# The eleventh image's store cut into one transfer of 60 rows and sixteen transfers of 4 rows, in a dilated convolution

## The chip, the core and the metric

The kernel runs on one NeuronCore of a Trainium2 chip. The metric is the device time of one execution in microseconds (us). Three runs of the kernel before gave 126.09, 126.11 and 126.12 us, median 126.11 us.

## The reference

The kernel computes a 3x3 convolution with dilation 2 and a padding of 2, so that the output has the size of the input. There are 16 images of 64 input channels and 64x64 pixels, 128 output channels, all in float32:

```python
for b in range(batch):
    for co in range(c_out):
        for ci in range(c_in):
            for kh in range(k):
                for kw in range(k):
                    output[b, co] += weight[co, ci, kh, kw] * x_pad[b, ci, kh*dilation:kh*dilation+h, kw*dilation:kw*dilation+w]
```

The output is 16 x 128 x 64 x 64 x 4 bytes = 33.55 MB, the input 16.8 MB. One image of the output is 2 MB, and it lies in a partition (an output channel) as 64 rows of 64 float32, 16,384 bytes in one piece, on the chip and in memory alike.

## The kernel before

**Work.** The images go in eight pairs, `pb` = 0 to 7. The two images of a pair sit on partitions 0 to 63 and 64 to 127, and a pair is worked in four units `u` of 16 rows each. For a unit, TensorE sums matmuls into PSUM (line 186), ScalarE copies the term that two row groups share to SBUF (line 204), and VectorE adds PSUM and copy into the output tile `o` (line 209), twice for each unit. GpSimd loads input pairs ahead of time (line 81) and adds up input rows (line 141).

**Output tiles.** `o` holds a whole pair, 128 partitions x 2 images x 64 x 64 float32. The pool `opool` has three buffers, so pair `pb` writes where pair `pb - 3` was, and has to wait until that one's store has landed.

**Stores.** All stores are issued by SyncE (SP) in the order of the program. Pairs 0 to 4 leave as one transfer of 4 MB each (line 221) once their last unit is added. Pairs 5 and 6 (`BOTH = NP - 3` is 5) leave as two transfers of 2 MB, one for each image (line 224, `hb` = 0 and 1). Pair 7 leaves in halves: after its second and after its fourth unit, two transfers of 1 MB. The eleventh image is image 10, `pb` = 5 with `hb` = 0. SP also issues three loads at the start: the weights (line 64) and the first pair of images in two parts (line 75). That makes 16 transfers on SP's queue.

**Completion semaphores.** A transfer tells of its landing by a semaphore that 16 shares add up to. The framework gives SP's transfers eight such semaphores in turn, called DMAHW0 to DMAHW7 in the built program. The ninth transfer gets the first one again, and SP does not issue it before the first transfer has landed; the tenth waits in the same way for the second one, and so on. The trace shows eight semaphore numbers, each used by two of the 16 transfers, and a wait for that number ahead of its second use. In the built program SP's list reads, from the last 4 MB store on:

```
L221 DMACopy out_0_dram<-o4_759 128x2x4096 [waits DVE_49]
L224 DMACopy out_0_dram<-o5_914 128x4096 [waits DMAHW0_49,DVE_49]
L224 DMACopy out_0_dram<-o5_914 128x4096 [waits DMAHW1_49]
L224 DMACopy out_0_dram<-o6_1070 128x4096 [waits DMAHW2_49,DVE_49]
L224 DMACopy out_0_dram<-o6_1070 128x4096 [waits DMAHW3_49]
```

The store of `o4` has DMAHW7; the three loads at the start have DMAHW0, 1 and 2.

Of the kernel before, what the change touches and what calls it, by code (L numbers as in the profile page):

```python
# [10 lines left out]
def kernel(  # L11
# [7 lines left out]
    nc = tc.nc  # L19

    B, CI, H, W = x.shape
# [56 lines left out]
    def load(pb, cuts):  # L78
        x16[pb] = x16pool.tile([P, H, W], f16, tag="x16", name=f"x16_{pb}")
        for lo, hi in zip(cuts, cuts[1:]):  # L80
            nc.gpsimd.dma_start(out=x16[pb][:, lo:hi], in_=x_pair[pb, :, lo:hi])  # L81
# [18 lines left out]
    for name, a in (("w21", 2), ("w01", 0)):  # L100
        for u in range(2):
            eng = nc.vector if name == "w21" else nc.gpsimd
            eng.tensor_sub(  # L103
                out=w16[:, SLOT[name] * KW : (SLOT[name] + 1) * KW, u, :],
# [8 lines left out]
    for n, name in enumerate(("w1", "w21", "w0", "w01", "w2")):  # L113
        ps = cpool.tile([P, 2, NB], f32, tag="ps", name=f"wt{n}")
        k0 = SLOT[name] * KW
        for j in range(KW):
            nc.tensor.matmul(  # L117
                out=ps[:, 0, j * CO : (j + 1) * CO],
# [16 lines left out]
    def prepare(pb, lo, hi):  # L135
        if pb not in s16:
            s16[pb] = sumpool.tile([P, 2 * NQ, W], f16, tag="s16", name=f"s16_{pb}")
        src = (x16[pb] if pb else x32).rearrange("p (q e r) w -> p q e (r w)", e=2, r=2)
        dst = s16[pb].rearrange("p (q r) w -> p q (r w)", r=2)
        q0, q1 = lo // 4, hi // 4  # L140
        nc.gpsimd.tensor_add(  # L141
            out=dst[:, q0:q1], in0=src[:, q0:q1, 0, :], in1=src[:, q0:q1, 1, :]
        )
# [37 lines left out]
    def phase(pb, u, terms):  # L181

        ps = cpool.tile([CO, 2, NB], f32, tag="ps", name="ps")
        for pair in zip(*(conv(pb, hb, ps[:, hb], u, terms) for hb in range(2))):
            for m in pair:
                nc.tensor.matmul(**m)  # L186
        return ps

    BOTH = NP - 3
    for pb in range(NP):  # L190
        o = opool.tile([P, 2, H, W], f32, tag="o", name=f"o{pb}")
        ov = o.rearrange("p b (q e r) w -> p b q e (r w)", e=2, r=2)
        for u in range(NU):

            if u == 1 and AHEAD <= pb + 2 < NP:
                load(pb + 2, [0, H])
            if pb + 1 < NP:
                if u == 1:
                    prepare(pb + 1, 0, 36)
                elif u == 2:  # L200
                    prepare(pb + 1, 36, H)

            s32 = spool.tile([P, 2, NB], f32, tag="s32", name="s32")
            nc.scalar.copy(out=s32, in_=phase(pb, u, [("w1", 2, 0)]))  # L204
            for e, terms in enumerate(
                ([("w21", 1, 0), ("w0", 1, -1)], [("w01", 0, 0), ("w2", 0, 1)])
            ):
                ps = phase(pb, u, terms)
                nc.vector.tensor_add(  # L209
                    out=ov[:, :, u * UQ : (u + 1) * UQ, e, :],  # L210
                    in0=ps.rearrange("p b (q c) -> p b q c", c=QW),
                    in1=s32.rearrange("p b (q c) -> p b q c", c=QW),
                )

            step = NU // 2 if pb == NP - 1 else NU
            if (u + 1) % step == 0:
                fl = slice((u + 1 - step) * 4 * UQ, (u + 1) * 4 * UQ)
                if pb < BOTH:  # L220
                    nc.sync.dma_start(out=out_pair[pb], in_=o)  # L221
                else:
                    for hb in range(2):
                        nc.sync.dma_start(out=out[2 * pb + hb, :, fl], in_=o[:, hb, fl])  # L224


# [33 lines left out]
```

## Time and profile before

The profile is of one execution. Its span, from the first to the last instruction, is 124.3 us; the median of the timed runs is 126.11 us.

| what | before |
|---|---|
| median of 3 runs | 126.11 us |
| span of the profiled execution | 124.3 us |
| TensorE (PE) busy | 105.2 us, 85% |
| VectorE (DVE) busy | 80.8 us, 65% |
| ScalarE (ACT) busy | 39.6 us, 32% |
| GpSimd (POOL) busy | 41.4 us, 33% |
| mean rate of the DMA engines | 349 GB/s |
| packets of SP's queue (q1) | 2944, 35.95 MB, 68.9% of 16 engines' span |
| last VectorE addition ends | 112.0 us |

The profile has one page with the busy shares, the span in 40 slices, the DMA queues, the chain of work that ended last, the groups of instructions and the issues of DMAs; and views that can be asked of the trace: who waited for whom, the instructions in order of time, busy time in stretches, and the records of single DMA packets and of the semaphore updates that tell of landings. A packet is one piece that one of the core's 16 DMA engines moves; a store of one whole image is 128 packets of 16,384 bytes, eight for each DMA engine. "Issue" is the time at which SP runs the DMA instruction, "landing" the last of its 16 semaphore updates.

### The profile page before, as it was taken

What the parts mean: (1) busy time and instruction counts of PE and PEld (TensorE: products, weight loads), DVE (VectorE), ACT (ScalarE), POOL (GpSimd) and SP (SyncE); (2) the same over time, 40 slices, a digit from 0 to 9 for tenths busy, and PEclk for the clock granted to TensorE, in tenths of its full rate; (3) what the DMA queues carried; (4) which work ended last, traced back from release to release, by engine and by line L of the source; (5) the groups of instructions that cost most, each with busy time, mean ns of one, the idle gap of its engine ahead of it and who ended that gap; (6) DMA issues with size and microseconds to landing.
All of it is one profiled execution on the core that took longest, in us unless ns stands there. A gap on an engine that the chain in (4) does not pass through costs nothing.

```text
span 124.3 us, 2244 instructions
## 1 busy us (share of the span) xinstructions
PE 105.2 (85%) x981; PEld 55.7 (45%) x981; DVE 80.8 (65%) x71; ACT 39.6 (32%) x40; POOL 41.4 (33%) x33
## 2 busy tenths in 40 slices
PE   6357999999999999999999999999999999960000
PEld 2043555555555555555555555555555555520000
DVE  0470199787778777877769778777877787770000
ACT  4760823333333333333333333333332433320000
POOL 2859998794095009500930093000000000000000
PEclk9999999999999999999999999999999999999655
DMA  4999999999999999999999999999999999999991
GB/s 129 346 359 218 214 214 216 224 237 411 393 327 314 332 306 319 316 390 314 324 345 427 425 427 432 422 427 427 432 438 427 432 414 432 427 417 419 422 406 71
DMA packets 3961, 43.42 MB, mean 349 GB/s; under 512 B 368, under 2 KB 368, under 8 KB 624
## 3 DMA queue, kind: packets, MB, share of 16 engines
q1 hardware_dynamic: 2944, 35.95, 68.9%
q0 software_dynamic: 1008, 7.34, 28.4%
q8 instruction: 7, 0.11, 0.3%
q14 instruction: 2, 0.02, 0.0%
HBM read 17.07 MB, written 33.55 MB: 407 GB/s over the span
## 4 chain that ended last, share of the span: by engine, by line
PE 80%; DMA 5%; POOL 2%; DVE 1%; DVEq 1%; SPq 0%; issue 0%
PE ps L186 80%; DMA x<-in_x_dram 5%; POOL s L141 2%; DVE o L209 1%; DVEq L255 1%; SPq L64 0%; DVEq L209 0%
## 5 line engine op out<-in xcount | busy, mean ns | idle before, releaser
L209 DVE TENSOR_TENSOR o<-ps,s 128x1024 f32<-128x1024 f32 x64 | 76.7, 1223 | 25.9 <-PE ps L186 16.8
L186 PE MATMUL ps<-x,w_sb 64*128 64x496 f16 (+3 forms) x768 | 85.3, 368 | 0.0
L186 PEld LDWEIGHTS <-w_sb 64*128 64x128 f16 x960 | 53.4, 95 | 49.3 <-issue 3.7
L204 ACT COPY s<-ps 128x1024 f32<-128x1024 f32 x32 | 32.4, 1012 | 63.0 <-PE ps L186 63.0
L141 POOL TENSOR_TENSOR s<-x 128x1152 f16<-128x1152 f16 (+4 forms) x18 | 35.1, 1971 | 31.1 <-PE ps L186 28.3
L186 PE MATMUL ps<-s,w_sb 64*128 64x496 f16 (+1 forms) x192 | 26.5, 379 | 2.1 <-POOL s L141 2.1
L81 POOL DMA_DIRECT2D x<-in_x_dram x7 | 4.0, 579 | 0.0
L132 ACT CAST x<-x 128x1024 f16<-128x1024 f32 (+1 forms) x3 | 2.8, 973 | 3.4 <-DMA x<-in_x_dram 3.4
L93 PE MATMUL warm<-zero 128*128 128x512 f16 x6 | 2.7, 630 | 1.2 <-DVE zero L87 1.2
L117 PE MATMUL wt<-ident,w 128*128 128x128 f16 x15 | 1.8, 312 | 2.1 <-ACT w L99 2.1
L103 DVE TENSOR_TENSOR w<-w 128x192 f16<-128x192 f32 x2 | 1.5, 800 | 2.5 <-DMA w<-in_weight_dram 2.5
L117 PEld LDWEIGHTS <-w 128*128 128x128 f16 x15 | 1.5, 146 | 3.0 <-ACT w L99 3.0
L99 ACT CAST w<-w 128x576 f16<-128x576 f32 x2 | 2.3, 1222 | 1.6 <-DMA w<-in_weight_dram 1.6
L103 POOL TENSOR_TENSOR w<-w 128x192 f16<-128x192 f32 x2 | 1.9, 951 | 2.4 <-DMA w<-in_weight_dram 2.4
L126 DVE CAST w_sb<-wt 128x384 f16<-128x384 f32 x3 | 1.6, 552 | 1.4 <-PE wt L117 1.4
L93 PEld LDWEIGHTS <-zero 128*128 128x128 f16 x6 | 0.7, 138 | 2.3 <-DVE zero L87 1.2
L99 ACT ACT_TABLE_LOAD x1 | 1.3, 1283 | 0.7 <-PEq L241 0.7
L128 ACT CAST w_sb<-wt 128x384 f16<-128x384 f32 x2 | 1.0, 478 | 1.1 <-PE wt L117 1.1
L130 DVE CAST x<-x 128x1280 f16<-128x1280 f32 x1 | 0.8, 826 | 0.5 <-DMA x<-in_x_dram 0.5
L87 DVE MEMSET zero<- 128x256 uint32 x1 | 0.3, 272 | 0.9 <-PEq L241 0.9
masks.py:199 POOL TENSOR_SCALAR_AFFINE_SELECT ident<-ident 128x128 f16<-128x128 f16 x1 | 0.3, 292 | 0.1
masks.py:197 POOL MEMSET ident<- 128x128 f16 x1 | 0.2, 204 | 0.3 <-POOLq L241 0.3
(4 smaller groups left out, 0.4 us busy)
## 6 DMA issues: line engine op xcount, KB each, us to landing
out_dram<-o SPq DMA_DIRECT2D x5, 4096.0 KB, 21.6
out_dram<-o SPq DMA_DIRECT2D x4, 2048.0 KB, 12.4
x<-in_x_dram POOLq DMA_DIRECT2D x7, 1024.0 KB, 16.0
out_dram<-o SPq DMA_DIRECT2D x4, 1024.0 KB, 10.6
x<-in_x_dram SPq DMA_DIRECT2D x1, 1152.0 KB, 6.5
x<-in_x_dram SPq DMA_DIRECT2D x1, 896.0 KB, 10.6
w<-in_weight_dram SPq DMA_DIRECT2D x1, 288.0 KB, 2.9
```

The costliest lines, as they stand in the source:

```text
L81: nc.gpsimd.dma_start(out=x16[pb][:, lo:hi], in_=x_pair[pb, :, lo:hi])
L93: nc.tensor.matmul(out=warm[:, 0], lhsT=zero[:, 0:P], rhs=zero, start=True, stop=True)
L99: nc.scalar.copy(out=w16[:, 0:NK, u, :], in_=w32k)
L103: eng.tensor_sub(out=w16[:, SLOT[name] * KW : (SLOT[name] + 1) * KW, u, :], in0=w32k[:, a * KW : (a + 1) * KW, :], in1=w32k[:, KW : 2 * KW ...
L117: nc.tensor.matmul(out=ps[:, 0, j * CO : (j + 1) * CO], lhsT=w16[:, k0 + j, :, :].rearrange("o t i -> o (t i)"), rhs=ident, start=True, st ...
L126: nc.vector.tensor_copy(out=dst, in_=ps[:, 0, 0 : KW * CO])
L132: nc.scalar.copy(out=x16[0][:, lo:hi], in_=x32[:, lo:hi])
L141: nc.gpsimd.tensor_add(out=dst[:, q0:q1], in0=src[:, q0:q1, 0, :], in1=src[:, q0:q1, 1, :])
L186: nc.tensor.matmul(**m)
L204: nc.scalar.copy(out=s32, in_=phase(pb, u, [("w1", 2, 0)]))
L209: nc.vector.tensor_add(out=ov[:, :, u * UQ : (u + 1) * UQ, e, :], in0=ps.rearrange("p b (q c) -> p b q c", c=QW), in1=s32.rearrange("p b ( ...
L255: with _tile.TileContext(nc) as tc:
```

## The change

The store of image 10 is cut. Rows 0 to 59 of all 128 partitions leave in one transfer. Rows 60 to 63, which are 1,024 bytes of each partition, leave in sixteen transfers of 15, 14, 13, ... 2, 1 and 8 partitions (together 128). The store of image 11 follows as before. Nothing is changed on the other engines.

```diff
     BOTH = NP - 3
+    STEPS = (*range(15, 0, -1), 8)
     for pb in range(NP):
...
                     for hb in range(2):
+                        if pb == BOTH and hb == 0:
+                            cut = H - 4
+                            nc.sync.dma_start(out=out[2 * pb, :, 0:cut], in_=o[:, 0, 0:cut])
+                            p0 = 0
+                            for n in STEPS:
+                                nc.sync.dma_start(
+                                    out=out[2 * pb, p0 : p0 + n, cut:H],
+                                    in_=o[p0 : p0 + n, 0, cut:H],
+                                )
+                                p0 += n
+                            continue
                         nc.sync.dma_start(out=out[2 * pb + hb, :, fl], in_=o[:, hb, fl])
```

SP's queue has 32 transfers now, and the eight semaphores go round four times. The built program's list from the last 4 MB store to the second store of pair 6, with the transfer's size and the semaphore waited for (each transfer then counts up that same semaphore):

```
L222 DMACopy out_0_dram<-o4_759 128x2x4096 [waits DVE_49]
L227 DMACopy out_0_dram<-o5_914 128x3840 [waits DMAHW0_49,DVE_49]
L230 DMACopy out_0_dram<-o5_914 15x256 [waits DMAHW1_49]
L230 DMACopy out_0_dram<-o5_914 14x256 [waits DMAHW2_49]
L230 DMACopy out_0_dram<-o5_914 13x256 [waits DMAHW3_49]
L230 DMACopy out_0_dram<-o5_914 12x256 [waits DMAHW4_49]
L230 DMACopy out_0_dram<-o5_914 11x256 [waits DMAHW5_49]
L230 DMACopy out_0_dram<-o5_914 10x256 [waits DMAHW6_49]
L230 DMACopy out_0_dram<-o5_914 9x256 [waits DMAHW7_49]
L230 DMACopy out_0_dram<-o5_914 8x256 [waits DMAHW0_49]
L230 DMACopy out_0_dram<-o5_914 7x256 [waits DMAHW1_49]
L230 DMACopy out_0_dram<-o5_914 6x256 [waits DMAHW2_49]
L230 DMACopy out_0_dram<-o5_914 5x256 [waits DMAHW3_49]
L230 DMACopy out_0_dram<-o5_914 4x256 [waits DMAHW4_49]
L230 DMACopy out_0_dram<-o5_914 3x256 [waits DMAHW5_49]
L230 DMACopy out_0_dram<-o5_914 2x256 [waits DMAHW6_49]
L230 DMACopy out_0_dram<-o5_914 1x256 [waits DMAHW7_49]
L230 DMACopy out_0_dram<-o5_914 8x256 [waits DMAHW0_49]
L236 DMACopy out_0_dram<-o5_914 128x4096 [waits DMAHW1_49]
L236 DMACopy out_0_dram<-o6_1086 128x4096 [waits DMAHW2_49,DVE_49]
L236 DMACopy out_0_dram<-o6_1086 128x4096 [waits DMAHW3_49]
```

The last wait value of each semaphore is that of its previous transfer: the transfer of 8 partitions that stands ninth waits until the transfer of 60 rows has landed in full.

## Prediction

> **What bounds the kernel now.** I read the span in slices first. TensorE is busy through to slice 36, but the rate of the DMA engines stands at 406 to 438 GB/s from slice 22 to slice 39, after the last arithmetic too, and it does not rise when TensorE stops:
>
> ```profile
> DMA  4999999999999999999999999999999999999991
> GB/s 129 346 359 218 214 214 216 224 237 411 393 327 314 332 306 319 316 390 314 324 345 427 425 427 432 422 427 427 432 438 427 432 414 432 427 417 419 422 406 71
> ```
>
> The page's chain of waits puts 80% on PE. It follows instructions and ends at the last addition, so it does not show what fills the time behind that. Busy time in stretches does (the columns after the engines are granted clock, DMA share and GB/s):
>
> ```profile
> 102.50:112.00 9.50, 8.16 (x80) 4.07 (x75) 7.26 (x7) 2.56 (x3) 0.00 (x0) 1.00 1.00 426
> 112.00:120.50 8.50, 0.00 (x0) 0.00 (x0) 0.01 (x1) 0.00 (x0) 0.00 (x0) 0.71 1.00 421
> 120.50:122.90 2.40, 0.00 (x0) 0.00 (x0) 0.00 (x0) 0.00 (x0) 0.00 (x0) 0.50 0.43 181
> 122.90:124.30 1.40, 0.00 (x0) 0.00 (x0) 0.00 (x0) 0.00 (x0) 0.00 (x0) 0.50 0.00 0
> ```
>
> The last addition ends at 112.0. For 8.5 us more all 16 DMA engines are full, for 2.4 us some have finished and others not, and 1.4 us are the end of the program. So the stores set the end, and from about 66 us a DMA engine that idles for 1 us brings 1 us, if it is the one that ends last. SP's own waits say the same: at the end it waits for landings, and for nothing else of length.
>
> ```profile
> SPq L255 <- DMA out_dram<-o: 9.2, 4, 2.4
> ```
>
> The packet records give the pace. A packet of 16,384 bytes starts 607 ns after the one before it, one of 8,192 bytes 306 ns, one of 2,304 bytes takes 91 ns at least: about 5 ns and 37 ns for each 1,024 bytes. Sorted by engine, the last share of each transfer ends as follows (first and last of the 16 DMA engines): pair 4 at 91.21 and 93.45, image 10 at 96.07 and 98.31, image 11 at 100.93 and 103.17, the last transfer at 120.55 and 122.90. Each engine goes from one packet to the next without a break, and keeps a lead or lag of up to 2.3 us. The page's issue rows show the backlog:
>
> ```profile
> out_dram<-o SPq DMA_DIRECT2D x5, 4096.0 KB, 21.6
> out_dram<-o SPq DMA_DIRECT2D x4, 2048.0 KB, 12.4
> ```
>
> A 2 MB store that takes the engines 4.86 us lands 12.4 us after its issue.
>
> **The change part by part.**
>
> *Bytes.* They are the same. The eight packets of each engine for image 10 shrink from 607 to about 5 + 15 x 37.6 = 569 ns, which gives 8 x 38 = 0.30 us back on every engine. The 128 small packets cost about 43 ns each, and each transfer adds a 4-byte semaphore packet that holds its engine 6 ns. On the mean engine this is 8 x 43 + 8.5 x 6 - 301 = +0.1 us.
>
> *What SP waits for.* This is the step that decides. The eight semaphores go round, and the list of the built program gives each transfer's predecessor. At 87.30 SP issues the 60 rows. The transfers of 15, 14 and 13 to 10 partitions wait for the first loads and the stores of pairs 0 to 3; the last of these landed at 84.2, so they go out at once. The transfer of 9 waits for pair 4, whose last semaphore update comes at 93.88 (issue 74.93, landing 18.9 us later). The next, of 8, waits until the 60 rows have landed. They stand behind pair 4 in every DMA engine: 93.45 + 8 x 0.569 = 98.0 on the last one, and 0.40 us from packet to semaphore (98.31 to 98.71 for image 10 before) gives **98.4**. Behind this waiting instruction stand eight more small transfers, then image 11 and all later stores. The engines, which before went on to image 11 between 96.07 and 98.31, run dry between 95.8 and 98.0, apart from some packets of 1 KB. No other work covers this: the loads end at 66 us.
>
> *What SP then issues.* From 98.4 nine small issues (8, 7, 6, 5, 4, 3, 2, 1, 8) stand ahead of image 11. The trace has no issue of so small a store. The rows that bound it:
>
> ```profile
> 0.74 0.37 SPq L64 DMA_DIRECT2D w<-in_weight_dram  x1
> 1.17 0.90 SPq L75 DMA_DIRECT2D x<-in_x_dram  x2
> ...
> L224 SPq DMA_DIRECT2D out_dram<-o x8: 332/730/1371, 87.3 to 112.4; - x8
> ```
>
> The loads at the start, with idle engines, follow each other at 0.43 and 0.47 us. Among the stores the first of a pair takes 0.33 to 0.34, the second, right behind it, 1.12 to 1.37 us. The low end is then 9 x 0.376 = 3.4 us, the high end 0.376 + 8 x 1.3 = 10.8 us. I take 0.45 for each, 4.05 us: at 98.4 the engines are idle as at the start, and the second stores of before follow a transfer of 128 partitions with the engines full, which these do not. Below the low end only a transfer with fewer partitions could be cheaper to issue; I give that 0.1 us for each, 1 us in all. The semaphores of the second round add nothing: image 11 waits for the transfer of 7, issued eight issues (3.6 us) earlier, and the weights' first shares landed 2.3 us after their issue.
>
> In a sentence by itself: the Trainium skill (DMA: Bandwidth & Descriptors, Rules for kernel authors) tells to join many small transfers, as below 64 KB it is mostly overhead, and its section on the anatomy of one DMA puts the fixed part at about 2.0 us for a transfer from GpSimd; nine of them in series would be an estimated 18 us, but the eight semaphores let them overlap, so that I count it for none.
>
> So image 11 is issued at 98.4 + 4.05 = 102.45. From issue to first packet on idle engines took 1.00 us for the weights (0.74 to 1.74), and the 16 engines began within 0.23 us. The first out store, 25.45 to 27.69, took 2.24 us, but among loads; this is the upper end, +1.2. I take 1.00: first packets from 103.45, on the last engine at **103.7**.
>
> *From there to the end.* Behind image 11 come the same bytes as before: three transfers of 2 MB and four of 1 MB. From the end of image 10 this took 24.5 us on the engine that was first (96.07 to 120.55) and 24.6 on the last one (98.31 to 122.90). The data of pairs 6 and 7 are there in time (112.0 for the last, which the engines reach at about 123), and SP's later waits are for small transfers that have landed. 103.7 + 24.5 = 128.2. The lag of 2.3 us is gone, since the engines begin anew together; this is why the loss is not the whole 7 us in which the first engine stands idle. On the last engine it is 128.2 - 122.9 = 5.3 us.
>
> *Other engines.* Pair 6 writes where pair 3 was, pair 7 where pair 4 was; both landings come ahead of the change. TensorE, VectorE, ScalarE and GpSimd keep their times.
>
> **Sum.** Span 124.26 + 5.3 = 129.6 us. The profiled span lies 1.85 us below the median of 126.11; with that kept, 126.11 + 5.3 = **131.4 us**.
>
> **The rivals.**
>
> *Dear issues.* Each issue behind another takes 1.25 to 1.3 us, as the second stores do, whatever its size. For it: all four second stores show it, and all of these carry a wait for a DMA semaphore in the same instruction, as the small ones do; the loads at the start carry none. Against it: it need not hold with idle engines and few partitions. Then image 11 is issued 6.7 us later: 98.4 + 10.8 = 109.2, and the time is 138.1.
>
> *The waits do not hold, and the steps even out the engines.* If image 11 reached the engines before they run dry, at 95.8 on the first and by 98 on the last, only the packets would count. If partition p of a small transfer goes to engine p, engine 0 gets 16 small packets and engine 15 none: 16 x 43 + 17 x 6 - 301 = +0.49 us on the one, -0.30 us on the other. The records do not number the engines. If those that lag are high ones, the time is 126.11 - 0.30 = 125.8, otherwise up to 126.6. It decides if SP issues image 11 by about 97. Against it: SP would have to pass the wait for the 60 rows, which cannot land before 98.0. The Trainium skill (DMA: Bandwidth & Descriptors, Why a DMA increments its semaphore by 16) has such a rule, the lowest-numbered engines as many as divide the partitions, and under Latency and other measured facts it calls engines 7 and 15 usually slower; the trace shows a fixed lag of some engines, and cannot tell which.
>
> *The change does not do what it says*, with the small packets spread over all engines: the waits are the same, and so is the time of the forecast.
>
> **How the numbers follow.** The forecast, with issues of 0.33 to 0.65 us and 1.0 to 1.6 us to the first packet, covers 130.2 to 133.8: 0.72. Dear issues, from there to 138.6: 0.21. The waits do not hold: 0.04, of which 0.03 faster. The remaining 0.03 is longer yet. The range runs from 130.0 (issues at 0.1 us less than the lowest row, in part) to 138.6 (dear issues, first packets half a microsecond later), and leaves out less than 2 in 10, as the two ends of the one unknown price lie 7 us apart. A measurement of this kernel can tell about 0.2% from no change: faster 0.03, same 0.01, slower 0.96.
>
> **What would show it.** In the profile after, the DMA shares should have a hole of some 5 to 7 us from about 96 to 103.5, with SP waiting for a landing from about 94.3 to 98.4 at the line of the small transfers; small issues of 0.45 us at most places; image 11 landing near 108.8; all 16 engines ending within 1 us of each other, and the last addition still at 112.0. Rates without a hole, or SP at image 11 before 97, would prove me wrong; a hole to 110 would be the first rival.

## The result and the profile after

The changed kernel takes 130.07 us (median of 4 runs, 129.98 to 130.70) against 126.12 us (126.09 to 126.81) beside it. The ratio is **1.029**, with a 95% interval of 1.0254 to 1.0326: slower, as forecast, but by 3.7 to 4.0 us and not by 5.3. The medians lie 3.95 us apart; the ratio gives 1.029 x 126.12 = 129.8 us, just under the range of the prediction, which began at 130.0.

The span of the profiled execution is 128.2 us. Its share of DMA time in 40 slices has a hole that was not there before, in the slices 30 and 31, counted from 0 (96.2 to 102.6 us):

```profile
DMA  4999999999999999999999999999992299999995
GB/s 140 360 348 215 210 210 225 217 279 435 363 337 299 332 319 332 353 358 304 330 394 424 437 429 419 424 455 409 423 410 73 93 409 470 429 409 409 409 427 227
```

Busy time in stretches places it. The columns behind the length are the five engines, then granted clock, DMA share and GB/s:

```profile
93.90:95.80 1.90, 1.90 (x22) 0.99 (x18) 1.35 (x2) 0.27 (x1) 0.00 (x0) 1.00 1.00 428
95.80:97.70 1.90, 1.90 (x22) 0.99 (x18) 1.10 (x2) 1.01 (x1) 0.00 (x0) 1.00 0.46 168
97.70:102.10 4.40, 4.40 (x49) 2.42 (x45) 3.96 (x4) 1.01 (x1) 0.00 (x0) 1.00 0.11 38
102.10:112.00 9.90, 8.89 (x86) 4.50 (x82) 7.66 (x7) 3.04 (x3) 0.00 (x0) 1.00 1.00 424
112.00:126.80 14.80, 0.00 (x0) 0.00 (x0) 0.34 (x1) 0.00 (x0) 0.00 (x0) 0.55 1.00 417
126.80:128.20 1.40, 0.00 (x0) 0.00 (x0) 0.00 (x0) 0.00 (x0) 0.00 (x0) 0.50 0.01 0
```

Up to 95.8 us the DMA engines are full. Then one after the other ends its rows of image 10, the last at 97.70; to 102.1 they do nearly nothing, while TensorE (the first number behind the length) works through without a break. From 102.1 to 126.8 they are full again, and there is no stretch at the end in which some have finished and others not, which before took 2.4 us: the packet records have the last shares at 126.81 to 126.97 (before 120.55 to 122.90).

SP's own waits name what held it. Line 230 is the small transfers:

```profile
SPq L230 <- DMA out_dram<-o: 2.5, 1, 2.5
```

One wait for a landing, 2.5 us, on a transfer that should only be issued. In order of time SP issues the 60 rows at 87.63 (0.33 us later than before, as the whole run is from its first stores on), then seven small transfers to 95.80; the eighth, of 8 partitions, waits to 98.29, when the 60 rows have landed (last semaphore update 98.28); image 11 is issued at 101.20 and its first packets start at 102.06 to 102.21. Four of the small issues (start and length in us):

```profile
88.02 1.20 SPq L230 DMA_DIRECT2D out_dram<-o  x1
...
92.67 1.12 SPq L230 DMA_DIRECT2D out_dram<-o  x1
...
98.29 0.28 SPq L230 DMA_DIRECT2D out_dram<-o  x1
...
100.59 0.25 SPq L230 DMA_DIRECT2D out_dram<-o  x1
```

The first six took 1.06 to 1.20 us each, while the DMA engines were full, the seventh 0.73 us just before they began to run dry, and those in the hole 0.25 to 0.30 us.

### The profile page after: what moved, and what is told of

It is laid out like the page before. It is cut to its first block, busy times and chain, and to the rows that moved or that the text cites. A ratio compares the mean times of both kernels' runs of the same rounds, so it can differ in the third digit from the quotient of the medians.

```text
span 128.2 us, 2260 instructions
## 1 busy us (share of the span) xinstructions
PE 105.7 (82%) x981; PEld 55.2 (43%) x981; DVE 81.0 (63%) x71; ACT 39.5 (31%) x40; POOL 41.5 (32%) x33
## 4 chain that ended last, share of the span: by engine, by line
PE 79%; DMA 4%; POOL 2%; DVE 1%; DVEq 1%; SPq 0%; issue 0%
PE ps L186 79%; DMA x<-in_x_dram 4%; POOL s L141 2%; DVE o L210 1%; DVEq L267 1%; SPq L64 0%; DVEq L210 0%
## 5 line engine op out<-in xcount | busy, mean ns | idle before, releaser
L186 PE MATMUL ps<-x,w_sb 64*128 64x496 f16 (+3 forms) x768 | 86.4, 371 | 0.0
L117 PE MATMUL wt<-ident,w 128*128 128x128 f16 x15 | 1.2, 219 | 2.3 <-ACT w L99 2.1
L117 PEld LDWEIGHTS <-w 128*128 128x128 f16 x15 | 0.9, 97 | 3.3 <-ACT w L99 3.0
```

Of the source, the lines that this page charges most:

```text
L117: nc.tensor.matmul(out=ps[:, 0, j * CO : (j + 1) * CO], lhsT=w16[:, k0 + j, :, :].rearrange("o t i -> o (t i)"), rhs=ident, start=True, st ...
```

## The experiments

The theory of the prediction: SP's eight semaphores go round, so the eighth small transfer waits for the landing of the 60 rows; image 11 stands behind it, and the DMA engines run dry. Two rivals were carried along. By the one, the small packets and transfers cost the time themselves. By the other, the issues do, at about 1.1 us each, whatever they wait for.

**Six small transfers, and seven.** Both send the same 128 packets of 1 KB. With six, image 11 takes over the semaphore of pair 4's store, which lands at about 93.9; with seven, that of the 60 rows.

```diff
-    STEPS = (*range(15, 0, -1), 8)
+    STEPS = (64, 32, 16, 8, 4, 4)         # six
+    STEPS = (64, 32, 16, 8, 4, 2, 2)      # seven
```

> Sixteen small transfers become six, of 64, 32, 16, 8, 4 and 4 partitions: the same 128 packets of 1 KB, but image 11 is now the eighth transfer after the store of pair 4 and waits for that one's landing (93.9 us), no longer for the 60 rows. Theory of the semaphore wait: SP reaches image 11 at about 94.4 to 95.5 us, the engines hardly run dry, 126.1 to 126.6 us. Rival of the packets (128 packets of 1 KB and their small transfers cost the time themselves): 129 to 130 us. Rival of the issue time (each issue takes 1.1 us while the engines are full, and only the number of issues counts): about the same as before, 126.1 to 126.6 us; the next kernel tells it from the first.

> Seven small transfers, of 64, 32, 16, 8, 4, 2 and 2 partitions: one more than in the kernel with six, and image 11 now waits for the landing of the 60 rows. Theory of the semaphore wait: image 11 is issued at 98.3 us, first packets at 99.2, all engines end together some 24.8 us later, 127.0 us (126.7 to 127.5). Rival of the issue time: one more issue of 1.1 us, image 11 at about 96 us and first packets at 96.9, within what the engines still have to do: 126.1 to 126.6 us. Rival of the packets: 129 to 130 us.

Six: 126.69 us, 1.0021 of the kernel before (0.9995 to 1.0047; before on this chip 126.50), so no difference that can be told. Seven: 128.07 us, 1.0128 (1.0102 to 1.0154). One more transfer (the last 4 partitions in two halves) costs 1.4 us. The DMA share (the number before the last) of the kernel with six, and then of the one with seven:

```profile
96.00:98.00 2.00, 1.00 1.07 436
98.00:100.00 2.00, 1.00 0.95 398
```

```profile
96.00:98.00 2.00, 1.00 0.67 257
98.00:100.00 2.00, 1.00 0.19 78
```

With six there is no hole, with seven there is one, and SP's waits of the latter have the cause at the line of image 11 (236):

```profile
SPq L236 <- DMA out_dram<-o: 3.2, 1, 3.2
```

The rival of the packets falls with six: the packets are all there. The rival of the issues falls with seven: the seventh small issue was over at 95.9, and by that rival image 11 would have gone out within some 1.1 us of it, yet it went out at 99.09. Seven came 0.6 us above the upper end of what was expected for it; SP issued the 60 rows at 88.29 in its profile, 1 us later than image 10 in that of before; they ended at 98.68 and not at 98.0, and the wait with them. The kernel with six also waits at line 236 (in all, number of waits, the longest):

```profile
SPq L236 <- DMA out_dram<-o: 4.0, 2, 3.7
```

The short wait, 0.3 us, is that of image 11 for pair 4's store. The long one is that of the first store of pair 6, which waits for the landing of the 60 rows before its own data are ready: nothing is queued behind it that the engines would need.

**The sixteen, issued by GpSimd.** Line 230 is taken out; the same transfers are issued on GpSimd after its row sums for pair 7 (`kept` is the tile of pair 5).

```diff
+                    if pb == BOTH + 1:
+                        p0 = 0
+                        for n in STEPS:
+                            nc.gpsimd.dma_start(
+                                out=out[2 * BOTH, p0 : p0 + n, H - 4 : H],
+                                in_=kept[p0 : p0 + n, 0, H - 4 : H],
+                            )
+                            p0 += n
```

> The sixteen transfers of 15 to 1 and 8 partitions stay as they are, but GpSimd issues them, after its last row sums for pair 7; SP goes from the 60 rows to image 11 at once. Theory of the semaphore wait: nothing holds SP, no hole in the DMA share, 126.1 to 126.8 us (the packets cost 0.1 us on the mean engine). Rival of the packets: 129 to 130 us. Rival of the issue time: no change either, since SP issues none of them.

127.70 us, 1.0108 (1.0067 to 1.0148). SP's list of waits has no landing any more except at the end (line 269). GpSimd's transfers go round on eight semaphores too, so now GpSimd waits at the line of the small transfers (206), and no large store stands behind it:

```profile
SPq L269 <- DMA out_dram<-o: 10.2, 5, 2.4
...
POOL out_dram L206 <- DMA out_dram<-o: 6.4, 6, 2.1
```

The DMA share shows no hole:

```profile
96.00:98.00 2.00, 1.00 1.00 419
98.00:100.00 2.00, 1.00 1.04 433
100.00:102.00 2.00, 1.00 0.99 403
```

So most of the loss goes, 2.3 us of 3.7. It is 0.9 us above the upper end of what was expected. From the end of pair 4's store to the end of the last one, the mean DMA engine took 29.61 us (before 29.45), the 0.1 to 0.2 us that the packets were priced at; but in this run pair 4's store ended 0.7 us later than in the profile of before (mean 92.91 against 92.19), and one engine ended 1.3 us after the next to last. What delayed pair 4's store is not settled; the late engine is taken up with the last two kernels.

**Sixteen transfers of 8 partitions, and the changed kernel again.** If the uneven steps made the loss, or held back a part of it, the even ones would show it.

```diff
-    STEPS = (*range(15, 0, -1), 8)
+    STEPS = (8,) * 16
```

> Sixteen transfers of 8 partitions each in place of 15, 14, ... 1 and 8: the same number of issues and of waits, another distribution over the DMA engines. Theory of the semaphore wait: the same hole and the same time as the changed kernel, 129.7 to 130.4 us. A theory by which the uneven steps (an engine with 16 small packets beside one with none) make the loss or hold back part of it: more than 0.4 us away from 130.0 us.

> The changed kernel once more, on the same chip as the next three. All theories: 130 us (129.7 to 130.8). It stands beside the kernel with sixteen transfers of 8 partitions (130.63 us, 1.0329 of the kernel before): if the uneven steps matter, this one should lie more than 0.4% of the kernel before away from 1.0329; by the theory of the semaphore wait the two ratios agree within 0.4%, as the wait ends when the slowest DMA engine has landed the 60 rows, which moves by about a microsecond from run to run.

The even steps took 130.63 us, 1.0329 (1.0303 to 1.0354), the changed kernel again 130.03 us, 1.0292 (1.0255 to 1.0329). They ran on two chips. The first was meant to be within 129.7 to 130.4 and missed this by 0.2 us; it lies 0.6 us from 130.0, more than the 0.4 us that were set as the mark of the uneven steps. That is why the changed kernel was run again: the two ratios lie within the 0.4% then allowed, at its edge. The traces tell where the difference is: the 60 rows ended at 98.55 with the even steps, at 97.76 with the uneven ones, and the waits at 98.95 and 98.33. From there the even steps went on as the others did, nine issues of 0.34 us on the mean. The steps do not make the loss; whether they change it by some tenths of a us cannot be told from these two kernels.

**Image 11 cut as well.** The condition loses `and hb == 0`, and `hb` stands in place of 0 in the tile's index.

```diff
-                        if pb == BOTH and hb == 0:
+                        if pb == BOTH:
```

> Image 11 is cut as image 10 is: 60 rows and then sixteen small transfers. Theory of the semaphore wait, with the lag of the engines given back once: a second hole from about 106.8 us, when the aligned engines end the 60 rows of image 11, to about 111.4 us, when the first store of pair 6 reaches them. There is no lag left to give back, so the second hole costs its whole width, 4.3 to 5.0 us, although it is narrower than the first (which was 6.3 us wide on the first engine and cost 4.0 us): 134.3 to 135.2 us. A rival by which the cost is simply the packets and issues, the same for each cut image: twice 4.0 us, 134.0 us or less. A rival by which the engines catch up in the shadow of the arithmetic: below 132 us.

134.93 us, 1.0673 (1.0639 to 1.0707), 4.9 us above the changed kernel on the same chip. The stretches have both holes:

```profile
96.00:102.00 6.00, 1.00 0.23 83
102.00:106.80 4.80, 1.00 0.86 361
106.80:112.30 5.50, 1.00 0.28 98
112.30:120.00 7.70, 0.67 1.00 421
```

In the profiled executions the two kernels lie 5.3 us apart (135.28 and 130.02). Of this 0.95 us belongs to the first hole, which ended later here: image 11 started on the DMA engines at 103.04, in the changed kernel at 102.09. The other 4.3 us are the second hole, from 107.73 to 108.05 on the engines' ends to 112.23 at the first store of pair 6. So the second hole cost its whole width, as expected. The first was some 7 us wide on the engine that ended first (96.12) and 4.3 us on the one that ended last (98.83); the engines ended the 60 rows of image 10 2.7 us apart and began image 11 within 0.15 us. That a hole costs what the last engine loses fits both. The rival with twice the same cost gives 134.0 us, below all four runs (134.73 to 135.28), but by less than the 0.95 us by which the first hole differed between two executions: this kernel alone does not rule it out.

**A split that relieves the engines from 8 on, and its control.** Both cut at row 56 and send the rest in three transfers, so that SP waits for nothing.

```diff
-                            cut = H - 4
+                            cut = H - 8
...
+    STEPS = (119, 8, 1)       # relieves
+    STEPS = (64, 32, 32)      # even, the control
```

> Three small transfers in place of sixteen, so no wait for the 60 rows, and rows 56 to 63 (2 KB of each partition) go to few engines on purpose: transfers of 119, 8 and 1 partitions. If a store uses as many of the lowest-numbered engines as divide its partitions, they run on 7, 8 and 1 engines, the engines 8 to 15 carry 16 KB less (0.6 us) and the engines 0 to 6 some 20 KB more (0.75 us). If the engines that lag are those from 8 on, as the small packets behind the 60 rows suggest (in the kernel with sixteen transfers of 8 partitions the five latest engines carried none), the last engine ends earlier: 0.3 to 0.6 us below the kernel with the even split, and up to 0.4% below the kernel before. If the lag is not tied to these engines: up to 0.7 us above the even split.

> The control for the one with 119, 8 and 1 partitions: the same 56 rows and three small transfers, of 64, 32 and 32 partitions, which use all 16 engines alike. Theory of the semaphore wait: no hole and no shift between engines, the time of the kernel before within 0.2%. Rival of the packets: 128 packets of 2 KB and three more transfers cost over 0.5%.

The relief took 127.40 us, 1.0078 (1.0052 to 1.0104), the control 127.20 us, 1.0051 (1.0027 to 1.0074). Neither hole nor wait is in either trace. The relief brought nothing: with 119, 8 and 1 the last shares ended at 120.87 to 123.84, with the even split at 120.81 to 123.89. That the control is 0.5% slower than before was not expected: the theory had allowed 0.2%, and 0.5% was where the rival of the packets began. Against that rival, its mean engine ended at 121.78 (before 121.64), as priced; its last one ended 1.45 us after the next.

The packet records show which engine that is. On one engine a packet starts when the one before it ends, so the records can be linked by their times. In every kernel here one engine takes some 630 to 670 ns for a packet of 16,384 bytes where the others take 611, from 67 or 68 us on, up to the hole where there is one and to about 111 us where there is none. In the five kernels without a hole this engine ends last: by 0.2 us in the kernel before, 0.7 with six transfers, 1.3 with GpSimd, 0.7 and 1.45 in the last two. The relief did not spare it: 18 small packets follow its 56 rows (97.25 to 98.76), with the even split 8 (98.14 to 98.82). What slows this engine stays open.

No kernel here beat the one before.

## Why the prediction was right in kind and wrong in size

*What bounds the kernel* held: a hole in the DMA share brought its width, less what the lag gave back, and TensorE had no part in it (its stretch through the hole is full, and the last addition ended at 112.3 instead of 112.0, by the run's 0.33 us).

*What SP waits for* held, to the transfer and to 0.1 us: the wait for the 60 rows ended at 98.29, forecast 98.4. Six and seven transfers show that this wait decides.

*What SP then issues* is the step that failed. "I take 0.45 for each, 4.05 us" measured 2.91 us (98.29 to 101.20), 0.32 for each. The row that I went by, the loads at the start, was that of transfers of 128 partitions; small stores with idle engines cost less than any row of before showed (0.25 to 0.30 us, against 0.33 at least). I had given that 0.1 us each below the lowest row and then let the range begin at 130.0 all the same. Taken through, 0.276 for each gives 1.57 us less than forecast, 129.8, and the range would have begun there.

*The first packet* came 0.86 us after the issue (taken: 1.00), within 0.15 us on all engines (0.23).

*To the end* it was 24.8 us on the last engine (102.21 to 126.97) instead of 24.5, so that of the 1.2 us between 128.2 and 126.97 the issues make 1.14, the wait 0.1, the first packets 0.2, and the pace takes 0.3 back. From 102 us on, with all engines level after the hole, a packet of 16,384 bytes took 620 ns on the mean, before 613.

*The lag* between the engines I had read as one that each engine keeps. For one engine that is wrong: the slow one of the last two kernels ended pair 4 in the profile of before at 92.66, 0.8 us ahead of the last, and the last transfer as the last, at 122.90. The forecast did not suffer by it, since the hole sets all engines level.

*The seven issues ahead of the wait* I had let go out "at once"; they took 7.8 us (88.02 to 95.80). It cost nothing, as the wait ended 2.5 us after them. SP waited from 95.8 instead of 94.3.

*Dear issues*, the first rival, had nearly its price where it did not count: the six small issues on full engines took 1.06 to 1.20 us (0.62 to 0.72 us for the same six in the kernel that cuts both images), and the nine that counted met idle ones. The same instruction form, with a semaphore wait in it, has both prices.

*The waits do not hold* did not happen. Its idea, to even out the engines by uneven shares, could be seen for itself in the relief, which gained nothing; the staircase of 15 to 1 itself, without the wait and on SP's queue, was not tried.

## What to carry to other kernels

Where a queue's completion semaphores go round, as the eight do here, count how many transfers stand between one and its predecessor on the same semaphore, and look at what the predecessor is queued behind. Here seven short transfers behind a long one were one too many, for everything behind them waited until the long one had landed. Price an issue by the state of the DMA engines and by what was issued just ahead of it: close behind another one and with full engines it mostly took 0.45 to 1.37 us (once 0.26, once 2.08), with idle engines or after a pause of 0.6 us or more 0.25 to 0.43 us.

## What the runs showed of the hardware that I had not expected

The issue's price hardly follows the size: behind another one on full engines a transfer of 4 partitions took 0.89 to 0.97 us and one of 64 partitions 0.94 us (kernel with six); on idle ones one of 1 partition took 0.25 us, one of 8 partitions 0.28 us and image 11 with 128 partitions 0.37 us. Full engines alone do not make it dear: the first store of a pair takes 0.33 us with full engines, and with sixteen transfers of 8 partitions the seventh, issued at 94.44 after a wait of 0.6 us, took 0.28 us while the DMA share stood at 0.95. What makes an issue dear was not tested by itself.

A small transfer behaves as one on few engines. After the issue of the 15 partitions at 88.02 its semaphore was updated once at 89.35, 6.5 us before any of its data moved (the first packet of 1 KB starts at 95.81), and then 15 times from 96.33 on. The Trainium skill (DMA: Bandwidth & Descriptors, Why a DMA increments its semaphore by 16 and not by 1) says that the sequencer writes the missing shares at once; the trace agrees, with 89.35.

The engine that ends the 60 rows last is not always the same. In the changed kernel it is the slow one (97.70), and 7 small packets follow on it. With sixteen transfers of 8 partitions and with both images cut another one is last, at 98.55 with none and at 98.83 with 1 small packet behind it; the slow one ends at 97.98 and 97.69, again with 7. Read by the rule of the lowest-numbered engines in the same section of the Trainium skill, 7 is an engine from 0 to 8 with the steps from 15 down, and one from 0 to 7 with the even ones, so that the slow engine can be the same each time. This is an inference from the order of packets; the records do not number the engines.
